# Seven-product FFN blocks: additions moved behind conversions, weight units taken earlier, two down products in the middle

## The chip, the cores and the metric

The kernel runs on one core of a Trainium2 chip. The metric is device time in microseconds (us) of one execution. TensorE (PE) multiplies, VectorE (DVE) and ScalarE (ACT) do elementwise work, SyncE (SP) issues the loads of weights.

## The reference

Two networks follow each other on x of 256 tokens by 1024. The first is an S5 block and an attention block. The second has two layers, each of an FFN, a hybrid mixer and another FFN:

```python
def swiglu(x, w_gate, w_up, w_down):
    return (jax.nn.silu(x @ w_gate) * (x @ w_up)) @ w_down
...
for l in range(DEPTH):
    x = x + 0.5 * swiglu(rmsnorm(x, ffn1_norm[l]), ffn1_w_gate[l], ffn1_w_up[l], ffn1_w_down[l])
    h = rmsnorm(x, mix_norm[l])
    x = x + hybrid_mixer(h, w_in[l], ...)
    x = x + 0.5 * swiglu(rmsnorm(x, ffn2_norm[l]), ffn2_w_gate[l], ffn2_w_up[l], ffn2_w_down[l])
return rmsnorm(x, final_norm)
```

The change is in the four FFNs: 1024 to 2816 and back to 1024, all in f32.

## The kernel before

**Products in three passes.** Every f32 operand is split into a high part (`whi`, written by ACT with a rounding copy, line 191) and a low part (`wlo`, what the copy left over, a subtraction on DVE, line 203). A product is then three matmuls on PE: high by high (line 280), then one with each low part (lines 281 and 282; in the FFN line 281 is the one that needs `wlo`).

**Units.** Weights come in units of 2048 columns per partition in all: four ACT copies of 512 and two DVE subtractions of 1024. `converting` is a generator over all units of the program; a step (a quarter) is one ACT copy, and the subtractions follow with a lag. `convert(n)` runs n steps, but stops once the unit after next is ready (`self.ready > self.taken + 2 - self.held`). `whi` and `wlo` have four buffers each, the loaded weights (`raw`) three. `take` hands over the next unit.

**Slots.** The program's order is written slot by slot. `K.slot` first issues the tasks due in the slot (on ACT and DVE), with `conv` conversion steps spread between them, and then the slot's matmuls with transposes (`pe`) at given places among them. An engine runs its instructions in the order issued here.

**An FFN.** The 2816 hidden columns are 11 blocks of 256. `BLOCKS = (1, 1, 1, 2, 1, 2, 1, 1, 1)` does seven blocks singly (`eight`: two slots of 24 matmuls) and twice a pair of blocks (`seven`): with sums and differences of the inputs (`xs`) and of four quarter blocks of weights (`Quad`, tiles `quad` and `mixed`, subtracted on DVE in `add`, line 168) seven products of 12 matmuls do the work of eight. Their sums are formed in the PSUM tiles a, b, c and, where two products share a tile, in SBUF: `sum11`, `sum22` and `sum12` (lines 581, 585, 589) are DVE additions. After a block is complete, `gated` makes silu(gate) on ACT (line 491) and multiplies on DVE (line 492), `turn` transposes on PE (line 498, tile `tph`), `divide` splits the result (tile `hh`), and a down product (`downs`, 24 matmuls into `acc`) adds it to the output. Down products of a block are done after the next block's `eight`, or inside the next `seven`: there the down product is cut in halves, one behind the fourth product and one behind the fifth.

The diff changes the order of all of these; the functions follow.

Of the kernel before, what the change touches and what calls it, by code (L numbers as in the profile page):

```python
# [14 lines left out]
ALU = mybir.AluOpType  # L15
# [3 lines left out]
P = 128  # L19
# [56 lines left out]
class Core:  # L76
# [20 lines left out]
    def f(self, shape, name, dtype=F32):  # L97
        return self.ap.tile(shape, dtype, tag="f", name=self.name(name), bufs=3)
# [132 lines left out]
        self.taken += 1  # L231
        return self.parts[i]

    def slot(self, mm, tasks=(), pe=(), conv=4):


        tasks = list(tasks)
        if conv > 2 and self.ready < self.taken + 2:
            conv += 2
        n = max(len(tasks), 1)  # L240
        done = 0
        for i in range(n):
            if i < len(tasks):
                tasks[i]()
            k = conv * (i + 1) // n
            self.convert(k - done)
            done = k
        if conv < 4:
            self.flush()
        pe = sorted(pe, key=lambda x: x[0])  # L250
        at = 0
        for _ in mm:
            while pe and pe[0][0] <= at:
                pe.pop(0)[1]()
            at += 1
        for _, f in pe:
            f()
# [187 lines left out]
BLOCKS = (1, 1, 1, 2, 1, 2, 1, 1, 1)  # L445


def ffn_units(w_gate, w_up, w_down):
    def quarter(j, k):
        cs = slice(j * 256, (j + 1) * 256)  # L450
        return [(0, w_gate[k * P:(k + 4) * P, cs]), (256, w_up[k * P:(k + 4) * P, cs])]

    out, j, due = [], 0, []
    assert sum(BLOCKS) == w_gate.shape[1] // 256 and BLOCKS[:2] == BLOCKS[-2:] == (1, 1)
    for b in BLOCKS:
        down = [(2, D, [(0, w_down[d * 256:(d + 1) * 256, :])]) for d in due]
        if b == 1:
            out += [(4, 512, quarter(j, k)) for k in (0, 4)] + down
        else:
            f = Quad([[quarter(j + i, k) for i in range(2)] for k in (0, 4)])  # L460
            out += f[:4] + down[:1] + f[4:5] + down[1:] + f[5:]
        due = list(range(j, j + b))
        j += b
    return out + [(2, D, [(0, w_down[d * 256:(d + 1) * 256, :])]) for d in due]


def ffn(K, h, norm, n, nxt):
# [3 lines left out]
    nc = K.nc  # L471
    V = nc.vector
    p, hid, tp, parts = {}, {}, {}, {}
    acc = []
    ahead = [([], []) for _ in range(3)]

    def slot(mm, tasks=(), pe=(), **kw):
        t, x = ahead.pop(0)
        ahead.append(([], []))
        K.slot(mm, t + list(tasks), x + list(pe), **kw)  # L480

    def then(i, *tasks, pe=()):

        ahead[i][0].extend(tasks)
        ahead[i][1].extend(pe)

    def gated(j, t, src=None):
        s = p[j][t] if src is None else src
        o = K.t([P, 512], "hid") if src is None or src is p.get((j, t)) else src
        a, hid[j, t] = o[:, 0:256], o[:, 256:512]  # L490
        nc.scalar.activation(a, s[:, 0:256], AF.Silu, scale=norm.col[:, t:t + 1])  # L491
        V.scalar_tensor_tensor(hid[j, t], s[:, 256:512], norm.col05[:, t:t + 1], a, op0=ALU.mult, op1=ALU.mult)  # L492

    def turn(j, t):
        if j not in tp:
            tp[j] = K.psum("ps", [P, 2, 2, P], "tph")
        for k in range(2):
            nc.tensor.transpose(tp[j][:, k, t], hid[j, t][:, k * P:(k + 1) * P], K.ident)  # L498

    def divide(j):  # L500
        hh = K.f([P, 2, 2, T], "hh", F32R)
        K.split(hh[:, 0], hh[:, 1], tp[j].rearrange("p k t c -> p k (t c)"))
        parts[j] = hh[:, 0], hh[:, 1]

    def down(j, w, hf, t):
        for k in range(2):
            c0 = hf * 512
            K.mm3(acc[hf][t], [a[:, k, t * P:(t + 1) * P] for a in parts[j]], [a[:, k, c0:c0 + 512] for a in w],
                  j == 0 and k == 0, j == n - 1 and k == 1)
            yield  # L510

    def downs(j, w, order=((0, 0), (0, 1), (1, 0), (1, 1))):
        for hf, t in order:
            yield from down(j, w, hf, t)
# [4 lines left out]
    def x_(hf, t):  # L519
        return [a[:, 4 * hf:4 * hf + 4, t * P:(t + 1) * P] for a in norm.x]  # L520
# [14 lines left out]
    def mix(i):  # L535
        f, s = blocks()
        a, b, op = ((f[1][0], f[1][1], ALU.add), (s[0], f[0][0], ALU.subtract), (f[0][0], f[1][0], ALU.subtract),
                    (f[0][1], s[1], ALU.subtract))[i]
        V.tensor_tensor(s[i], a, b, op=op)
# [9 lines left out]
    def s_(i):  # L549
        return [a[:, i] for a in sums["x"]]  # L550

    def form(out, a, first=False):

        w = K.take()
        for k in range(4):
            K.mm3(out, [y[:, k] for y in a], [y[:, k] for y in w], first and k == 0, k == 3, not first)
            yield

    def eight(j, due):

        p[j] = K.pair()
        for kh in range(2):
            tasks, pe = [], []
            if j == 0 and kh == 0:
                pe = norm.begin(1)
            elif j == 0:
                tasks = [norm.col_, norm.half_col]
            slot(K.rows_of(p[j], norm.x, K.take(), 4 * kh, 4, kh == 0, kh == 1), tasks, pe,
                 conv=2 if j == 0 and kh == 0 else 4)
        places = (3, 5) if due else (5, 7)  # L570
        then(0, lambda: gated(j, 0), lambda: gated(j, 1), pe=[(x, lambda t=t: turn(j, t)) for t, x in enumerate(places)])
        then(1, lambda: divide(j))

    def seven(j, due):

        a, b, c = (K.psum("ps", [P, 512], "p") for _ in range(3))
        c11, u2 = K.t([P, 512], "hid"), K.t([P, 512], "hid")
        c22 = K.t([P, 512], "hid")

        def sum11():  # L580
            V.tensor_tensor(c11, c11, b, op=ALU.add)
            gated(j, 0, c11)

        def sum22():
            V.tensor_tensor(c22, c22, a, op=ALU.add)
            gated(j + 1, 1, c22)

        def sum12():
            V.tensor_tensor(u2, u2, c, op=ALU.add)
            gated(j + 1, 0, u2)  # L590

        def sum21():
            p[j, 1] = a
            gated(j, 1, a)

        slot(form(a, x_(0, 0), first=True))
        then(0, lambda: nc.scalar.copy(c11, a))
        slot(form(b, x_(1, 0), first=True))
        then(0, sum11)
        slot(form(c, s_(0), first=True))  # L600
        then(0, lambda: nc.scalar.copy(c22, c))
        slot(form(a, s_(1)))
        then(0, lambda: nc.scalar.copy(u2, a))
        w = K.take()
        K.held = 1
        if len(due) == 1:
            slot(downs(due[0], w, ((0, 0), (0, 1))))
        else:
            slot(downs(due[0], w))
            K.held = 0  # L610
        slot(form(a, s_(2)))
        then(0, sum22)
        if len(due) == 1:
            slot(downs(due[0], w, ((1, 0), (1, 1))))
            K.held = 0
        else:
            slot(downs(due[1], K.take()))
        slot(form(a, x_(1, 1)))
        then(0, sum21)
        slot(form(c, s_(3)))  # L620
        then(0, sum12, pe=[(2, lambda: turn(j, 0)), (2, lambda: turn(j, 1)), (4, lambda: turn(j + 1, 1)),
                           (6, lambda: turn(j + 1, 0))])
        then(1, lambda: divide(j), lambda: divide(j + 1))

    j, due = 0, []
    for b in BLOCKS[:-1]:
        if b == 1:
            eight(j, due)
            if j == 0:
                then(1, whole)  # L630
            elif j == 1:
                acc = [K.pair("acc", "acc") for _ in range(2)]
                then(0, lambda: mix(0), lambda: mix(1))
                then(1, lambda: mix(2), lambda: mix(3), mixed_high, mixed_low)
            for d in due:
                slot(downs(d, K.take()))
        else:
            seven(j, due)
        due = list(range(j, j + b))
        j += b  # L640
    j = n - 1
    eight(j, due)
    ahead[0] = ([], [])
    ahead[1] = ([], [])
    w = [K.take()]

    def turned():
# [1496 lines left out]
```

## Time and profile before

| | |
|---|---|
| median of 3 runs | 1431.38 us (1429.34 to 1433.12) |
| profiled execution | 1432.99 us, of which its span is 1431.0 us |
| PE busy | 1377.9 us (96%) |
| DVE busy | 1103.0 us (77%) |
| ACT busy | 814.4 us (57%) |
| mean granted TensorE clock | 0.989 |

Busy time is summed over stages with different limits. Ends of matmuls are modelled, so that PE's own pace is read from the starts of its instructions. In a timeline a row has start, duration, engine, line, operation, tiles (written<-read), shapes and, in brackets, the idle time of the engine before it and what ended this.

### The profile page before, as it was taken

To read this page: it belongs to the slowest core of one execution; us is meant where nothing else is said; L and a number is where in the kernel's file an instruction comes from. 1 tells how busy PE (TensorE), PEld (TensorE's weight loads), DVE (VectorE), ACT (ScalarE), POOL (GpSimd) and SP (SyncE) were. 2 spreads that over 40 slices of the span, in tenths; PEclk is the share of its full clock that TensorE was granted. 3 is DMA by queue.
4 is the path that set the end of the run, shared out by engine and by line. 5 is a ranking of instruction groups with operands and counts; after the bars stand their busy time and mean duration, and the time that the engine had idled before them with its cause. 6 is when DMAs were issued, how large, how long until landed. Compare 5 with 4: busy or idle time off the path is not lost.

```text
span 1431.0 us, 21193 instructions
## 1 busy us (share of the span) xinstructions
PE 1377.9 (96%) x8205; PEld 1151.2 (80%) x8205; DVE 1103.0 (77%) x1801; ACT 814.4 (57%) x1581; POOL 28.1 (2%) x35
## 2 busy tenths in 40 slices
PE   8988999999999999999999999999999999999996
PEld 7877888988778899888877788787889887878775
DVE  7889887668886589777878747887669987688854
ACT  6525657665655474555565636566557564656552
POOL 0003200000000000000000000000000000000000
PEclk9999999999999999999999999999999999999998
DMA  8133655466446454465726556473645445646260
GB/s 211 63 123 104 213 172 154 139 199 215 150 144 235 148 177 141 132 196 164 257 80 214 186 169 203 150 236 98 228 131 191 147 170 170 213 147 230 85 215 29
DMA packets 181347, 237.16 MB, mean 166 GB/s; under 512 B 16952, under 2 KB 140144, under 8 KB 181248
## 3 DMA queue, kind: packets, MB, share of 16 engines
q1 hardware_dynamic: 180160, 233.47, 50.2%
q0 software_dynamic: 672, 1.81, 0.4%
q8 instruction: 64, 1.05, 0.3%
q10 hardware_dynamic: 416, 0.55, 0.1%
q14 instruction: 35, 0.29, 0.1%
HBM read 234.76 MB, written 1.05 MB: 165 GB/s over the span
## 4 chain that ended last, share of the span: by engine, by line
PE 79%; DVE 12%; DMA 2%; issue 2%; ACT 2%; SPq 0%; DVEq 0%; ACTq 0%
PE p L280 15%; PE p L281 15%; PE p L282 15%; PE acc L281 5%; PE acc L282 5%; PE acc L280 5%; DVE wlo L203 4%; PE g L281 2%; PE g L280 2%; PE g L282 2%; DVE quad L168 2%; DMA raw<-in_ffn_w_up_dram 1%; PE lv L1712 1%; PE tph L498 1%; PE g L764 1%
## 5 line engine op out<-in xcount | busy, mean ns | idle before, releaser
L191 ACT CAST whi<-raw 128x512 fp32r<-128x512 f32 x688 | 381.7, 619 | 151.3 <-PE p L282 81.7
L203 DVE TENSOR_TENSOR wlo<-raw,whi 128x1024 fp32r<-128x1024 f32 x344 | 410.5, 1217 | 7.6 <-ACT whi L191 7.2
L280 PE MATMUL p<-whi,xghi 128*128 128x512 f32 x800 | 319.9, 400 | 0.0
L281 PE MATMUL p<-wlo,xghi 128*128 128x512 f32 x800 | 312.8, 391 | 0.3
L282 PE MATMUL p<-whi,xglo 128*128 128x512 f32 x800 | 312.5, 391 | 0.0
L281 PEld LDWEIGHTS p<-wlo,xghi 128*128 128x128 f32 x800 | 150.5, 188 | 32.6 <-DVE wlo L203 3.6
L282 PEld LDWEIGHTS p<-whi,xglo 128*128 128x128 f32 x800 | 150.2, 188 | 32.1
L280 PEld LDWEIGHTS p<-whi,xghi 128*128 128x128 f32 x800 | 150.3, 188 | 29.0
L281 PE MATMUL acc<-wlo,hh 128*128 128x512 f32 x352 | 141.8, 403 | 15.4 <-DVE wlo L203 15.4
L280 PE MATMUL acc<-whi,hh 128*128 128x512 f32 x352 | 144.5, 410 | 0.0
L282 PE MATMUL acc<-whi,hh 128*128 128x512 f32 x352 | 140.7, 400 | 0.0
L191 ACT CAST whi<-quad 128x512 fp32r<-128x512 f32 x192 | 107.9, 617 | 52.3 <-DVE quad L168 29.7
L203 DVE TENSOR_TENSOR wlo<-quad,whi 128x1024 fp32r<-128x1024 f32 x96 | 113.6, 1217 | 0.0
L281 PEld LDWEIGHTS acc<-wlo,hh 128*128 128x128 f32 x352 | 67.6, 192 | 34.1 <-DVE wlo L203 22.3
L492 DVE SCALAR_TENSOR_TENSOR hid<-p,col,hid 128x256 f32<-128x256 f32 x64 | 30.8, 481 | 68.7 <-ACT hid L491 68.6
L282 PEld LDWEIGHTS acc<-whi,hh 128*128 128x128 f32 x352 | 67.5, 192 | 15.6 <-DVE hh L294 1.7
L280 PEld LDWEIGHTS acc<-whi,hh 128*128 128x128 f32 x352 | 67.2, 191 | 13.9 <-ACT hh L293 1.6
L294 DVE TENSOR_TENSOR hh<-tph,hh 128x512 fp32r<-128x512 f32 x44 | 30.4, 691 | 58.6 <-ACT hh L293 58.2
L280 PE MATMUL g<-xghi,whi 128*128 128x256 f32 x256 | 73.8, 288 | 0.0
L282 PE MATMUL g<-xghi,wlo 128*128 128x256 f32 x256 | 72.4, 283 | 0.0
L281 PE MATMUL g<-xglo,whi 128*128 128x256 f32 x256 | 72.4, 283 | 0.0
L764 PE MATMUL g<-xg,raw 128*128 128x256 f32 x256 | 61.0, 395 | 5.5 <-DVE kt L1043 3.6
(377 smaller groups left out, 2249.1 us busy)
## 6 DMA issues: line engine op xcount, KB each, us to landing
raw<-in_ffn_w_down_dram SPq DMA_DIRECT2D x44, 1024.0 KB, 4.9
raw<-in_w_in_dram SPq DMA_DIRECT2D x36, 1024.0 KB, 5.1
raw<-in_ffn_w_gate_dram SPq DMA_DIRECT2D x56, 512.0 KB, 4.1
raw<-in_ffn_w_up_dram SPq DMA_DIRECT2D x56, 512.0 KB, 5.2
raw<-in_attn_w_in_dram SPq DMA_DIRECT2D x16, 1024.0 KB, 5.6
quad<-in_ffn_w_gate_dram SPq DMA_DIRECT2D x32, 512.0 KB, 9.2
quad<-in_ffn_w_up_dram SPq DMA_DIRECT2D x32, 512.0 KB, 8.7
raw<-in_w_out_dram SPq DMA_DIRECT2D x8, 1024.0 KB, 5.1
```

Source lines behind the costliest of these rows:

```text
L168: self.nc.vector.tensor_tensor(u.buffer(self)[:, sl], a, b, op=ALU.subtract)
L191: self.nc.scalar.copy(hf[:, sl], raw[:, sl])
L203: self.nc.vector.tensor_tensor(out, raw, hi.bitcast(F32), op=ALU.subtract)
L280: nc.tensor.matmul(out, ah, bh, start=start, stop=False, skip_group_check=more)
L281: nc.tensor.matmul(out, ah, bl, start=False, stop=False, skip_group_check=more)
L282: nc.tensor.matmul(out, al, bh, start=False, stop=stop, skip_group_check=more)
L294: self.nc.vector.tensor_tensor(lo, x, hi.bitcast(F32), op=ALU.subtract)
L492: V.scalar_tensor_tensor(hid[j, t], s[:, 256:512], norm.col05[:, t:t + 1], a, op0=ALU.mult, op1=ALU.mult)
L498: nc.tensor.transpose(tp[j][:, k, t], hid[j, t][:, k * P:(k + 1) * P], K.ident)
L764: nc.tensor.matmul(us[s][:, m], ws[s][:, k, m * P:(m + 1) * P], xg[:, k], start=k == 0, stop=k == KC - 1)
L1712: nc.tensor.matmul(o, e[:, sl], e[:, sl], start=True, stop=True)
```

## The change

Four edits, all of order:

- `slot` takes a list `late`: the tasks of the slot are issued first, then half of its conversion steps, then the late tasks with the other half. `sum11`, `sum22`, `sum12` and the gating of the fourth output (`sum21`) become late tasks.
- Slots of an FFN have `conv=8` instead of 4 (or 6), and `seven` takes a unit ahead of its slot's conversions instead of behind them, so that conversions run one unit further ahead.
- `sum22` no longer reads a from PSUM: ACT copies a into a new tile u3 first.
- `kept_back`: of the down products due ahead of a `seven`, the last stays back, so that every `seven` has two whole down products in its middle and the `eight` before it one less behind it. Where none is left behind an `eight`, its transposes move into the second slot of the `seven`. The loads of the down weights move behind those of the quads.

```diff
-    def slot(self, mm, tasks=(), pe=(), conv=4):
+    def slot(self, mm, tasks=(), pe=(), conv=4, late=()):
         tasks = list(tasks)
-        if conv > 2 and self.ready < self.taken + 2:
+        if late:
+            for f in tasks:
+                f()
+            self.convert(conv // 2)
+            tasks = list(late)
+            conv -= conv // 2
+        if 2 < conv <= 4 and self.ready < self.taken + 2:
             conv += 2
...
+def kept_back(i, due):
+    return due[-1:] if i + 1 < len(BLOCKS) and BLOCKS[i + 1] == 2 else []
...
         if b == 1:
-            out += [(4, 512, quarter(j, k)) for k in (0, 4)] + down
+            kept = kept_back(i, due)
+            out += [(4, 512, quarter(j, k)) for k in (0, 4)] + down[:len(due) - len(kept)]
...
-        due = list(range(j, j + b))
+        due = kept + list(range(j, j + b))
...
-    def slot(mm, tasks=(), pe=(), **kw):
+    def slot(mm, tasks=(), pe=(), conv=8):
...
-        places = (3, 5) if due else (5, 7)
-        then(0, lambda: gated(j, 0), lambda: gated(j, 1), pe=[(x, lambda t=t: turn(j, t)) for t, x in enumerate(places)])
-        then(1, lambda: divide(j))
+        gates, turns = [lambda: gated(j, 0), lambda: gated(j, 1)], [lambda: turn(j, 0), lambda: turn(j, 1)]
+        then(0, *gates)
+        if n_downs:
+            then(0, pe=list(zip((3, 5), turns)))
+            then(1, lambda: divide(j))
...
+        else:
+            then(1, pe=list(zip((1, 2), turns)))
+            then(2, lambda: divide(j))
...
-            V.tensor_tensor(c22, c22, a, op=ALU.add)
+            V.tensor_tensor(c22, c22, u3, op=ALU.add)
...
-        slot(form(b, x_(1, 0), first=True))
-        then(0, sum11)
+        slot(form(b, x_(1, 0), K.take(), True))
+        then(0, late=[sum11])
...
-        slot(form(a, s_(2)))
-        then(0, sum22)
+        slot(form(a, s_(2), K.take()))
+        copy(u3, a)
+        then(0, late=[sum22])
```

Three places show what moves. Line numbers of the changed kernel are larger (581 is 601 there, 492 is 506, 498 is 512).

**DVE, first block of seven products of the first FFN, around `sum11`** (tile `hid_480`, after the change `hid_474`). Before:

```order
L168 TENSOR_TENSOR mixed_475_3758<-quad_444_3543,quad_441_3534 128x1024
L203 TENSOR_TENSOR wlo_473_3750<-quad_441_3534,whi_472_3749 128x1024 x2
L581 TENSOR_TENSOR hid_480_3795<-hid_480_3795,p_478_3793 128x512
L492 SCALAR_TENSOR_TENSOR hid_480_3795<-hid_480_3795,col05_432_3483 128x256
L203 TENSOR_TENSOR wlo_485_3815<-mixed_475_3758,whi_484_3814 128x1024
L168 TENSOR_TENSOR quad_443_3540<-quad_444_3543,quad_443_3540 128x1024
```

After:

```order
L203 TENSOR_TENSOR wlo_480_3757<-mixed_470_3717,whi_479_3756 128x1024
L168 TENSOR_TENSOR quad_436_3498<-quad_437_3501,quad_436_3498 128x1024
L203 TENSOR_TENSOR wlo_480_3757<-mixed_470_3717,whi_479_3756 128x1024
L301 TENSOR_TENSOR hh_485_3807<-tph_484_3796,hh_485_3807 128x512
L168 TENSOR_TENSOR quad_436_3498<-quad_437_3501,quad_436_3498 128x1024
L203 TENSOR_TENSOR wlo_483_3782<-raw_443_3541,whi_482_3781 128x1024 x2
L601 TENSOR_TENSOR hid_474_3749<-hid_474_3749,p_472_3747 128x512
L506 SCALAR_TENSOR_TENSOR hid_474_3749<-hid_474_3749,col05_432_3484 128x256
```

The addition waits for the block's second product (`p_478`, now `p_472`). The conversions of the fourth unit (`mixed`), of the fifth's first difference and of a down unit stood behind it or later and now stand ahead of it.

**DVE, ahead of the same block, around the gating of the single block before it** (tiles `hid_478` and `hid_481`, its two halves), after the change:

```order
L506 SCALAR_TENSOR_TENSOR hid_478_3753<-p_461_3667,col05_432_3484,hid_478_3753 128x256
L168 TENSOR_TENSOR mixed_470_3717<-quad_437_3501,quad_434_3492 128x1024
L203 TENSOR_TENSOR wlo_469_3712<-quad_434_3492,whi_468_3711 128x1024 x2
L506 SCALAR_TENSOR_TENSOR hid_481_3765<-p_462_3668,col05_432_3484,hid_481_3765 128x256
L203 TENSOR_TENSOR wlo_480_3757<-mixed_470_3717,whi_479_3756 128x1024
```

Before, two operations stood between the two halves; now three do, and the stretch of conversions ahead of them is another one, since the down unit that was converted there comes later.

**PE, second product of the same block, after the change** (`p_472` is b; `tph_484` takes the transposes of the single block before):

```order
L512 MATMUL tph_484_3796<-ident_67,hid_478_3753 128x128 x2
L287 MATMUL p_472_3747<-whi_464_3672,xghi_410_3345 128x512
L288 MATMUL p_472_3747<-wlo_465_3673,xghi_410_3345 128x512
L289 MATMUL p_472_3747<-whi_464_3672,xglo_411_3346 128x512
L512 MATMUL tph_484_3796<-ident_67,hid_481_3765 128x128 x2
```

These transposes stood between the matmuls of the down product that came ahead of the block; that product now stands inside the block, and they stand behind the second product's sixth and ninth matmul.

## Rows read from the trace of the kernel before

**Rows 1.** The profile's page: span, and busy time of each engine.

```profile
span 1431.0 us, 21193 instructions
PE 1377.9 (96%) x8205; PEld 1151.2 (80%) x8205; DVE 1103.0 (77%) x1801; ACT 814.4 (57%) x1581; POOL 28.1 (2%) x35
```

**Rows 2.** Windows: two of eight seven-product blocks, the eight's sum, a stretch inside.

```profile
349.06:379.15 30.09, 27.42 (x109) 20.96 (x108) 23.74 (x25) 17.95 (x34) 0.00 (x0) 0.94 0.11 36
402.44:431.33 28.89, 26.25 (x110) 19.81 (x108) 24.14 (x25) 17.96 (x34) 2.12 (x4) 1.00 0.19 66
sum 236.44, PE 215.12 PEld 163.30 DVE 191.56 ACT 143.65 POOL 4.24; mean PE 26.89 PEld 20.41 DVE 23.94 ACT 17.96 POOL 0.53
361.26:367.94 6.68, 4.76 (x13) 3.17 (x12) 6.64 (x6) 3.76 (x7) 0.00 (x0) 0.74 0.36 100
```

**Rows 3.** Waits, whole program: us in total, times, longest us.

```profile
PE acc L281 <- DVE wlo L203: 15.4, 16, 1.3
PE tph L498 <- DVE hid L492: 2.0, 3, 0.8
DVE hid L581 <- PE p L282: 16.1, 8, 3.1
DVE hid L585 <- PE p L282: 19.4, 8, 3.1
ACT whi L191 <- PE p L282: 88.9, 36, 3.5
```

**Rows 4.** Timeline, TensorE, first block: start us, duration us, what.

```profile
343.10 0.39 PE L280 MATMUL acc<-whi,hh 128*128 128x512 f32 x1
349.06 0.39 PE L280 MATMUL p<-whi,xghi 128*128 128x512 f32 x1
...
362.27 0.50 PE L281 MATMUL acc<-wlo,hh 128*128 128x512 f32 x1 [0.61 <-DVE wlo L203]
...
364.55 0.80 PE L281 MATMUL acc<-wlo,hh 128*128 128x512 f32 x1 [1.31 <-DVE wlo L203]
...
367.94 0.39 PE L280 MATMUL p<-whi,xshi 128*128 128x512 f32 x1
...
370.66 0.39 PE L280 MATMUL acc<-whi,hh 128*128 128x512 f32 x1
```

**Rows 5.** Timeline, VectorE, same stretch.

```profile
354.79 0.69 DVE L581 TENSOR_TENSOR hid<-hid,p 128x512 f32<-128x512 f32 x1 [2.23 <-PE p L282]
356.06 0.48 DVE L492 SCALAR_TENSOR_TENSOR hid<-hid,col 128x256 f32<-128x256 f32 x1 [0.58 <-ACT hid L491]
356.46 1.22 DVE L203 TENSOR_TENSOR wlo<-mixed,whi 128x1024 fp32r<-128x1024 f32 x1
357.60 1.22 DVE L168 TENSOR_TENSOR quad<-quad,quad 128x1024 f32<-128x1024 f32 x1
...
365.55 2.35 DVE L203 TENSOR_TENSOR wlo<-quad,whi 128x1024 fp32r<-128x1024 f32 x2
```

**Rows 6.** Timeline, VectorE, ahead of that block.

```profile
321.59 0.69 DVE L294 TENSOR_TENSOR hh<-tph,hh 128x512 fp32r<-128x512 f32 x1 [3.32 <-ACT hh L293]
...
331.65 0.69 DVE L294 TENSOR_TENSOR hh<-tph,hh 128x512 fp32r<-128x512 f32 x1
...
335.52 2.29 DVE L547 TENSOR_TENSOR xslo<-xs,xshi 128x2048 fp32r<-128x2048 f32 x1 [0.85 <-ACT xshi L543]
```

**Rows 7.** Groups by line: busy us, mean ns, idle before.

```profile
L203 DVE TENSOR_TENSOR wlo<-raw,whi 128x1024 fp32r<-128x1024 f32 x344 | 410.5, 1217 | 7.6 <-ACT whi L191 7.2
```

**Rows 8.** Timeline, ScalarE then TensorE, behind a second block.

```profile
1370.33 1.14 ACT L191 CAST whi<-raw 128x512 fp32r<-128x512 f32 x2 [2.07 <-DMA raw<-in_ffn_w_up_dram]
...
1372.41 0.44 PE L498 MATMUL tph<-ident,hid 128*128 128x128 f32 x2 [0.81 <-DVE hid L492]
```

**Rows 9.** Page, DMA issues: KB each, median us to landing.

```profile
raw<-in_ffn_w_down_dram SPq DMA_DIRECT2D x44, 1024.0 KB, 4.9
quad<-in_ffn_w_gate_dram SPq DMA_DIRECT2D x32, 512.0 KB, 9.2
```

More of the change, by code (lines that the diff above doesn't have):

```diff
@@ L454, in ffn_units @@
     assert sum(BLOCKS) == w_gate.shape[1] // 256 and BLOCKS[:2] == BLOCKS[-2:] == (1, 1)
-    for b in BLOCKS:
+    for i, b in enumerate(BLOCKS):
         down = [(2, D, [(0, w_down[d * 256:(d + 1) * 256, :])]) for d in due]
+        kept = []
         if b == 1:
-            out += [(4, 512, quarter(j, k)) for k in (0, 4)] + down
+            kept = kept_back(i, due)
+            out += [(4, 512, quarter(j, k)) for k in (0, 4)] + down[:len(due) - len(kept)]
         else:
@@ L474, in ffn, with then @@
     acc = []
-    ahead = [([], []) for _ in range(3)]
-    def slot(mm, tasks=(), pe=(), **kw):
[L478 to L485, printed above, removed]
+    ahead = [([], [], []) for _ in range(3)]
+    def slot(mm, tasks=(), pe=(), conv=8):
+        t, x, late = ahead.pop(0)
+        ahead.append(([], [], []))
+        K.slot(mm, t + list(tasks), x + list(pe), conv, late)
+    def then(i, *tasks, pe=(), late=()):
+        for x, y in zip(ahead[i], (tasks, pe, late)):
+            x.extend(y)
     def gated(j, t, src=None):
@@ L550, in s_, with form @@
         return [a[:, i] for a in sums["x"]]
-    def form(out, a, first=False):
-        w = K.take()
+    def form(out, a, w, first=False):
         for k in range(4):
@@ L557, in form, with eight @@
             yield
-    def eight(j, due):
+    def eight(j, n_downs):
         p[j] = K.pair()
@@ L568, in eight @@
             slot(K.rows_of(p[j], norm.x, K.take(), 4 * kh, 4, kh == 0, kh == 1), tasks, pe,
-                 conv=2 if j == 0 and kh == 0 else 4)
-        places = (3, 5) if due else (5, 7)
-        then(0, lambda: gated(j, 0), lambda: gated(j, 1), pe=[(x, lambda t=t: turn(j, t)) for t, x in enumerate(places)])
-        then(1, lambda: divide(j))
+                 conv=2 if j == 0 and kh == 0 else 8)
+        gates, turns = [lambda: gated(j, 0), lambda: gated(j, 1)], [lambda: turn(j, 0), lambda: turn(j, 1)]
[3 more added lines that the diff above has]
+            then(1, lambda: divide(j))
+        elif j == 0:
+            then(0, pe=list(zip((5, 7), turns)))
+            then(1, lambda: divide(j))
+        else:
+            then(1, pe=list(zip((1, 2), turns)))
+            then(2, lambda: divide(j))
     def seven(j, due):
         a, b, c = (K.psum("ps", [P, 512], "p") for _ in range(3))
-        c11, u2 = K.t([P, 512], "hid"), K.t([P, 512], "hid")
-        c22 = K.t([P, 512], "hid")
+        c11, u2, c22, u3 = (K.t([P, 512], "hid") for _ in range(4))
         def sum11():
@@ L594, in sum21, with copy @@
             gated(j, 1, a)
-        slot(form(a, x_(0, 0), first=True))
-        then(0, lambda: nc.scalar.copy(c11, a))
-        slot(form(b, x_(1, 0), first=True))
-        then(0, sum11)
[L600 to L603, printed above, removed]
+        def copy(dst, src):
+            then(0, lambda: nc.scalar.copy(dst, src))
+        slot(form(a, x_(0, 0), K.take(), True))
+        copy(c11, a)
+        slot(form(b, x_(1, 0), K.take(), True))
+        then(0, late=[sum11])
+        slot(form(c, s_(0), K.take(), True))
+        copy(c22, c)
+        slot(form(a, s_(1), K.take()))
+        copy(u2, a)
         w = K.take()
-        K.held = 1
+        halves = (((0, 0), (0, 1)), ((1, 0), (1, 1)))
         if len(due) == 1:
-            slot(downs(due[0], w, ((0, 0), (0, 1))))
+            K.held = 1
+            slot(downs(due[0], w, halves[0]))
         else:
             slot(downs(due[0], w))
-            K.held = 0
-        slot(form(a, s_(2)))
-        then(0, sum22)
+        slot(form(a, s_(2), K.take()))
+        copy(u3, a)
+        then(0, late=[sum22])
         if len(due) == 1:
-            slot(downs(due[0], w, ((1, 0), (1, 1))))
+            slot(downs(due[0], w, halves[1]))
             K.held = 0
@@ L617, in seven @@
             slot(downs(due[1], K.take()))
[L618 to L622, printed above, removed]
+        slot(form(a, x_(1, 1), K.take()))
+        then(0, late=[sum21])
+        slot(form(c, s_(3), K.take()))
+        then(0, late=[sum12], pe=[(2, lambda: turn(j, 0)), (2, lambda: turn(j, 1)), (4, lambda: turn(j + 1, 1)),
+                           (7, lambda: turn(j + 1, 0))])
         then(1, lambda: divide(j), lambda: divide(j + 1))
     j, due = 0, []
-    for b in BLOCKS[:-1]:
+    for i, b in enumerate(BLOCKS[:-1]):
         if b == 1:
-            eight(j, due)
+            kept = kept_back(i, due)
+            eight(j, len(due) - len(kept))
             if j == 0:
@@ L634, in ffn @@
                 then(1, lambda: mix(2), lambda: mix(3), mixed_high, mixed_low)
-            for d in due:
+            for d in due[:len(due) - len(kept)]:
                 slot(downs(d, K.take()))
@@ L638, in ffn @@
             seven(j, due)
-        due = list(range(j, j + b))
+            kept = []
+        due = kept + list(range(j, j + b))
         j += b
     j = n - 1
-    eight(j, due)
-    ahead[0] = ([], [])
-    ahead[1] = ([], [])
+    eight(j, 1)
+    ahead[0] = ([], [], [])
+    ahead[1] = ([], [], [])
     w = [K.take()]
```

## Prediction

> **What bounds the kernel now.** I read the page first, then the waits, then windows and timelines of the stretch that the change touches. On the page PE is busy for 96% of the span and the next engine, DVE, for 77% [rows 1]: a gain must come out of the gaps of PE. The waits say where those are: PE in a down product waits for the low part of weights, `wlo`, in 16 waits of up to 1.3 us [rows 3]. Sixteen is two for each of the eight blocks of seven products (two in each of four FFNs), so I went there.
>
> The price of a block comes from its windows. Twelve matmuls without a gap take 370.66 - 367.94 = 2.72 us [rows 4], 0.2267 us each. A block before the change has 7 products and one down product, 9 x 12 = 108 matmuls, so 24.5 us. The first takes 30.09 us, the second 28.89, all eight 236.44 [rows 2]: 236.44 - 8 x 24.48 = **40.6 us** are lost in the eight blocks. I use this difference and not the idle times of the waits, which start at modelled ends of matmuls and come out smaller.
>
> The two shown blocks differ by 1.2 us and in the granted clock, 0.94 against 1.00; the stretch behind the long waits has 0.74 [rows 2], so the clock there was at 1.2 instead of 2.4 GHz for a part. That came after gaps of PE that ended at 362.27 and 364.55 [rows 4]. It is a consequence of the waits, and in the sum above.
>
> Why is `wlo` late? DVE is busy for only 23.74 of 30.09 us [rows 2]. Its timeline shows `sum11` (L581) waiting 2.23 us for a product of PE, and the multiplication behind it another 0.58 us for ACT [rows 5]. DVE runs its queue in order, so the conversions behind these two stand still. From 356.46 to the end of the pair at 365.55, about 367.9, DVE then runs without a gap, in steps of 357.60 - 356.46 = 1.14 us per 1024 columns [rows 5] (1217 ns each, which overlap a little [rows 7]), and PE waits for it. Later `sum22` (L585) does the same: 19.4 us in 8 waits, `sum11` 16.1 in 8 [rows 3]. So DVE is idle while work for PE is behind it in its queue, then it is the bound for 11 us.
>
> **The change, part by part.**
>
> *Late additions.* Half of the slot's conversions go ahead of `sum11`, which is asked for at the end of the second product. In the new order six conversions or differences stand between the previous gating and it, 6 x 1.14 = 6.8 us: DVE reaches it when its product is done. Worth, per block: the 2.23 us of idle time and what follows from it. The 0.58 us for ACT stays; it delays everything behind it once.
>
> *Two whole down products instead of one.* PE gets 24 matmuls more in the block, 5.4 us, and DVE the two low parts of one more unit, 2 x 1.14 = 2.3 us. Over the FFN nothing is added, since both are missing behind the single block ahead. In the block it gives DVE 5.4 - 2.3 = 3.1 us in which to catch up.
>
> *Units taken ahead.* Conversion runs one unit further ahead. Nothing costs PE here as long as buffers are free; an ACT copy into the fourth buffer waits for the product that reads it (88.9 us in 36 waits already now [rows 3]), and what stands behind it in ACT's queue waits too. The gating's second half is such an instruction: it now stands behind four copies instead of two, two steps of 0.5 us later.
>
> *The copy u3.* Eight ACT copies more in the program, half a us each, in slots in which ACT (17.95 of 30.09 us [rows 2]) has room: nothing. Without that room it would delay the copies behind it by that half us.
>
> *The moved transposes: a new wait.* Where no down product is left ahead of the first block of an FFN, the transposes of the single block before come after the sixth and ninth matmul of the second product. I count when DVE has their input. Before, the block before ended at 343.10 [rows 4]; the new order puts the seven products there. The last event that the change doesn't move is the `hh` of 321.59, over at 322.2 [rows 6]. From there to the second half of the gating the new order has 16 operations of 1024 columns (18.2 us at 1.14), four of 512 and one `hh` (0.6 us each, 3.1), three multiplications (0.4 each by 356.46 - 356.06 [rows 5], 1.2) and the 2048-wide `xslo` (2.2): 24.7 us. Two waits remain: until 331.65 for the next `hh`, which DVE now reaches 0.6 us early, and 0.85 for `xshi` [rows 6]. So it starts at 322.2 + 24.7 + 1.4 = 348.3 and ends at 348.8. PE asks for it after 12 + 9 matmuls and a pair of transposes: 343.10 + 21 x 0.2267 + 0.15 = 348.0. PE waits **0.8 us**. A DVE without those two waits would give 0, one that is a further 2 us late 2.8.
>
> Then DVE has, without a gap, two low parts and two differences of 1024, one `hh` and the down unit's two low parts, 6 x 1.14 + 0.6: the second of these is done at about 356.2. PE wants it after three more matmuls, two products and four matmuls of the down product: 355.1 + 0.9 = 356.0. That is 0.2 to 0.3 us late; counting on through `sum11` and four conversions, the second down unit is as late again. I take 1.4 us for the first block of an FFN. Ahead of the second block a down product remains, and by the same count its units are 1 to 2 us early; I take 0.4 there. Per FFN 1.8 us, in the program 4 x 1.8 = **7.2 us** of waits that come or stay.
>
> *Behind the second block.* There the gating stands behind a copy that waits 2.07 us for weights, and PE's transposes wait 0.81 us for it [rows 8]; 2.0 us in three such waits [rows 3]. With units converted earlier the loads are asked for earlier. I take half, 1.0 us, between 0 and 2.
>
> *The loads.* In SP's queue the held down unit now stands behind eight loads of the quads. A load lands 4.9 us after its issue, one of a quad 9.2 [rows 9]. The quads must be there for the block's first products; the down unit is wanted four products, 10.9 us, after the first of these, so I take nothing. Without that room a copy would wait, as in the slower rival below.
>
> The sum, on the profiled execution's 1433.0 us (1.6 above the median of the three runs): 1433.0 - 40.6 - 1.0 + 7.2 = 1398.6; against the median, **1397 us**. Waits at zero everywhere would give 1431.4 - 40.6 - 2.0 = 1389.
>
> **The rivals.**
>
> *DVE stays late.* For it: from the gating to the end of the block DVE has some 20 operations in a row without a gap, and each us by which it starts late is a us of PE in the block; the gaps may again bring the clock down. Against it: DVE is busy for 79% of a block now. If it is 2 us later than counted in all eight blocks, 16 us of the gain go: 1413. It decides against the forecast from a second gating half at 350 on.
>
> *Nothing moves, since it isn't the order.* What would make this so is a buffer: if `wlo` were late because its four buffers free up late, the order would not matter and the time stay 1431. The 88.9 us of copies that wait for PE [rows 3] speak for it. Against it speaks that DVE's conversions run gap to gap from 356.46 and wait for no buffer [rows 5]. The Trainium skill has this as a rule (Perfetto Trace Analysis, Optimization Strategy): the same gap repeated on the engine that should be full can mean too few SBUF or PSUM buffers. Our gap repeats eight times, but the rows name a late operand, so by the trace the rule does not hold for these gaps.
>
> *Slower: the weights come late.* The second block's down units are loaded behind all its quads, and those wait until the first block has let go of its own. If a down unit landed after its slot began, ACT's whole queue would stand behind its copy. Its buffer comes free when the single block's first unit is converted, and its copy is due three slots of 24 matmuls and a product later, 3 x 5.44 + 2.72 = 19 us, against 9.2 us for a load among others [rows 9]. To lose, each of eight blocks must wait 34.4 / 8 = 4.3 us, so a load must take over 23 us. Every further us costs 8: at 25 us the time is 1397 + 8 x 6 = 1445.
>
> **How the numbers follow.** The forecast (1389 to 1404) has 0.66, DVE late (1404 to 1418) 0.22, a smaller gain from both 0.04, nothing 0.05, slower 0.03. The likeliest case gives 1397. The range 1388 to 1412 leaves out less than 2 in 10: its lower end is all waits gone, its upper DVE late by nearly 2 us in each block. Differences of under 0.3%, 4 us, are about what a measurement of this kernel can't tell from none. Faster by more: 0.92; within: 0.05; slower: 0.03.
>
> **What would show it.** In the profile after, `sum11` and `sum22` should have no wait for PE, and the 15.4 us of PE in down products for `wlo` should fall under 4. A window of a block, now 132 matmuls or 29.9 us, should take 30 to 32 us, at a granted clock of 1.00. PE's transposes should show four waits for the multiplication of about 0.8 us, one per FFN, in the first blocks; were these 2 us or more, or the clock still lower there, the count of DVE's operations is wrong. Waits of ACT for loads of down weights over 2 us would be the third rival.

## The result and the profile after

The changed kernel takes 1394.28 us (median of 4 runs, 1393.96 to 1396.21); the kernel before, run beside it, 1432.22 us. The ratio is 0.9741, with a 95% interval of 0.9724 to 0.9759. By the ratio it is faster by 37 us. The forecast was 1397 us.

The page after, span and busy times; its profiled execution took 1394.2 us:

```profile
span 1392.1 us, 21232 instructions
PE 1360.4 (98%) x8205; PEld 1148.8 (83%) x8205; DVE 1101.1 (79%) x1801; ACT 817.5 (59%) x1589; POOL 27.4 (2%) x35
```

Against [rows 1] the span is 38.9 us shorter, DVE has as much work as before (1101.1 us) and ACT has 8 instructions more, the copies u3. PE runs as many instructions as before. What was saved is waiting, and the stretches at the lower clock that came with it.

Windows of the eight blocks of seven products, each from its first matmul to the first one behind it (duration, busy time of PE, PEld, DVE, ACT and POOL, then clock, DMA share, GB/s). A block now has 132 matmuls, 29.92 us without a gap:

```profile
341.32:373.20 31.88, 31.13 (x138) 24.89 (x136) 30.72 (x32) 23.36 (x45) 0.00 (x0) 1.00 0.40 131
391.10:421.04 29.94, 29.94 (x133) 24.77 (x132) 28.39 (x28) 22.69 (x43) 2.12 (x4) 1.00 0.27 83
697.10:729.02 31.92, 31.17 (x138) 24.90 (x137) 30.77 (x32) 23.39 (x45) 0.00 (x0) 1.00 0.41 129
746.90:776.84 29.94, 29.94 (x133) 24.78 (x132) 28.39 (x28) 22.68 (x43) 0.00 (x0) 1.00 0.26 82
880.86:912.77 31.91, 31.19 (x138) 24.89 (x136) 30.75 (x32) 23.38 (x45) 0.00 (x0) 1.00 0.41 131
930.64:960.58 29.94, 29.94 (x134) 24.77 (x133) 28.40 (x28) 22.70 (x43) 2.12 (x4) 1.00 0.26 83
1236.69:1268.56 31.87, 31.15 (x138) 24.90 (x137) 30.71 (x32) 23.36 (x45) 0.00 (x0) 1.00 0.40 131
1286.42:1316.88 30.46, 30.44 (x134) 24.63 (x133) 28.43 (x28) 23.02 (x44) 0.00 (x0) 1.00 0.24 71
sum 247.86, PE 244.90 PEld 198.54 DVE 236.55 ACT 184.58 POOL 4.24; mean PE 30.61 PEld 24.82 DVE 29.57 ACT 23.07 POOL 0.53
```

Three of the four second blocks have almost no gap left (0.02 us over 29.92). Every window has the clock 1.00, where the first of [rows 2] had 0.94. And DVE is now busy for 30.72 of 31.88 us in a first block: it has room of about a microsecond.

Waits of TensorE over the whole program (us in total, times, longest):

```profile
PE tph L512 <- DVE hid L506: 3.1, 5, 0.7
PE yps L1090 <- issue: 0.6, 2, 0.4
```

The second row is the shortest that this view gives; a down product's wait for `wlo`, 15.4 us in [rows 3], is no longer among its rows. The waits for the gating have grown in number, from 3 to 5: the four new ones that were forecast, and one of the three old ones. TensorE, second product of the first block:

```profile
346.09 0.39 PE L289 MATMUL p<-whi,xglo 128*128 128x512 f32 x1
347.21 0.44 PE L512 MATMUL tph<-ident,hid 128*128 128x128 f32 x2 [0.73 <-DVE hid L506]
347.40 0.48 PE L287 MATMUL p<-whi,xghi 128*128 128x512 f32 x1
...
348.18 0.40 PE L287 MATMUL p<-whi,xshi 128*128 128x512 f32 x1
```

VectorE, same stretch, to be read beside [rows 5]:

```profile
346.68 0.47 DVE L506 SCALAR_TENSOR_TENSOR hid<-p,col,hid 128x256 f32<-128x256 f32 x1
347.07 1.21 DVE L203 TENSOR_TENSOR wlo<-mixed,whi 128x1024 fp32r<-128x1024 f32 x1
...
352.21 2.35 DVE L203 TENSOR_TENSOR wlo<-raw,whi 128x1024 fp32r<-128x1024 f32 x2
354.48 0.68 DVE L601 TENSOR_TENSOR hid<-hid,p 128x512 f32<-128x512 f32 x1
355.74 0.48 DVE L506 SCALAR_TENSOR_TENSOR hid<-hid,col 128x256 f32<-128x256 f32 x1 [0.58 <-ACT hid L505]
356.14 1.22 DVE L203 TENSOR_TENSOR wlo<-quad,whi 128x1024 fp32r<-128x1024 f32 x1
```

`sum11` (L601) has no bracket: its 2.23 us of waiting for PE are gone. It now starts 6.3 us after the next product began at 348.18, so the product that it adds is long done; the 0.58 us behind it for ACT stayed.

**Where the time came from.** The eight windows exceed 8 x 29.92 us by 8.5 us. Of these, 16 transposes, which stood outside the block before, are 1.9: eight pairs of 0.23 us each (from 341.32 to 346.09 there are 20 steps of 0.2267 us and one pair). So 6.6 us are lost where 40.6 were: 34.0 us. Behind the second blocks, the next 96 matmuls with their transposes take 93.6 us in the four FFNs together, where they took 96.5: 2.9 us. That is 36.9 of the 38.9 us by which the span fell. Of the other 2.0 us, 1.8 were gained ahead of the first block (it starts at 341.32, and before, the down product in that place started at 343.10). They need not come from the change: in the run with both gating halves early (below), whose order up to this block is the same, it starts at 343.77.

### The profile page after: what moved, and what is told of

It reads as the page before. It is cut to its first block, busy times and chain, and to the rows that moved or that the text cites. A ratio compares the mean times of both kernels' runs of the same rounds, so it can differ in the third digit from the quotient of the medians.

```text
span 1392.1 us, 21232 instructions
## 1 busy us (share of the span) xinstructions
PE 1360.4 (98%) x8205; PEld 1148.8 (83%) x8205; DVE 1101.1 (79%) x1801; ACT 817.5 (59%) x1589; POOL 27.4 (2%) x35
## 5 line engine op out<-in xcount | busy, mean ns | idle before, releaser
L287 PE MATMUL acc<-whi,hh 128*128 128x512 f32 x352 | 141.7, 402 | 0.0
L288 PE MATMUL acc<-wlo,hh 128*128 128x512 f32 x352 | 138.7, 394 | 0.1
L289 PE MATMUL acc<-whi,hh 128*128 128x512 f32 x352 | 138.1, 392 | 0.0
L289 PEld LDWEIGHTS acc<-whi,hh 128*128 128x128 f32 x352 | 66.1, 188 | 15.4 <-DVE hh L301 1.7
```

Of the source, the lines that this page charges most:

```text
L287: nc.tensor.matmul(out, ah, bh, start=start, stop=False, skip_group_check=more)
L288: nc.tensor.matmul(out, ah, bl, start=False, stop=False, skip_group_check=more)
L289: nc.tensor.matmul(out, al, bh, start=False, stop=stop, skip_group_check=more)
```

## Experiments

The three parts were first made alone on the kernel before, then taken out of the kernel after one at a time, and then the one surprise was taken apart. Ratios are to the kernel before:

| kernel | median us | ratio (95% interval) |
|---|---|---|
| before + late additions only | 1416.35 | 0.9897 (0.9880 to 0.9915) |
| before + two whole down products only | 1416.69 | 0.9900 (0.9882 to 0.9918) |
| before + further reach only | 1410.04 | 0.9852 (0.9835 to 0.9869) |
| after without late additions | 1397.25 | 0.9766 (0.9747 to 0.9784) |
| after, unit taken behind its slot's conversions | 1411.12 | 0.9861 (0.9840 to 0.9883) |
| after without u3 | 1397.87 | 0.9766 (0.9751 to 0.9781) |
| after, halves of one down product | 1422.90 | 0.9942 (0.9925 to 0.9958) |
| the same, copy of a ahead of four casts | 1411.68 | 0.9866 (0.9851 to 0.9880) |
| the same, additions ahead of conversions | 1412.57 | 0.9865 (0.9849 to 0.9882) |
| after, both gating halves early | 1395.64 | 0.9750 (0.9735 to 0.9765) |

The theory was that the order of DVE's queue makes `wlo` late. The main rival was that DVE has too much to do in a block whatever the order, the other that buffers decide.

**Late additions alone.**

```diff
-        then(0, sum11)
+        then(0, late=[sum11])
```

(and the same for `sum22`, `sum21` and `sum12`, with `late` in `slot` as in the change.)

> The kernel before with one edit: the four additions of a seven-product block go behind half of their slot's conversions; order of units, reach of the conversions and down products as before. Theory (DVE idles at the head of its queue for sum11, and its conversions are late for it): the 2.2 us of waiting ahead of sum11 become about 0, the waits of PE in a block fall from 4.4-5.6 to about 2.5 us, the time to 1408-1415. Rival (VectorE has too much to do in the block, whatever the order): the waits of PE stay, 1428-1432.

It gained 15 us, and at 1416 us lies 1 us above the theory's range. Its waits of TensorE:

```profile
PE acc L288 <- DVE wlo L203: 15.3, 16, 1.3
PE tph L505 <- DVE hid L499: 0.4, 1, 0.4
```

The wait for `wlo` in down products is as large as in [rows 3], and yet the blocks were 27.5 us where 28.9 and 30.1 were (three with a fallen clock 28.8). The transposes' wait for the gating fell from 2.0 us to 0.4. What went inside the blocks is a gap of 0.8 us (from start to start) in the fourth product, ahead of those in the down product. The waits of before have it in a row that [rows 3] leaves out, and this run does not have it:

```profile
PE p L281 <- DVE wlo L203: 4.8, 8, 0.6
```

The down product's waits stayed although `sum11` waits for nothing now. VectorE in the first block, first a row of before, then three of this run:

```profile
361.00 1.22 DVE L203 TENSOR_TENSOR wlo<-raw,whi 128x1024 fp32r<-128x1024 f32 x1
```

```profile
353.24 0.68 DVE L588 TENSOR_TENSOR hid<-hid,p 128x512 f32<-128x512 f32 x1
...
358.40 1.22 DVE L203 TENSOR_TENSOR wlo<-raw,whi 128x1024 fp32r<-128x1024 f32 x1
...
360.67 1.22 DVE L203 TENSOR_TENSOR wlo<-raw,whi 128x1024 fp32r<-128x1024 f32 x1
```

The down unit's first low part is made 2.6 us earlier, but PE comes to it 2.6 us earlier too (its wait ends at 359.67, in [rows 4] at 362.27). DVE runs without a gap from 355.00 on, and between the two low parts it still makes a difference of quads. So the idle time of DVE at `sum11` cost time, but not in the row on which I had put it.

**Two whole down products alone.**

```diff
-            out += [(4, 512, quarter(j, k)) for k in (0, 4)] + down
+            kept = kept_back(i, due)
+            out += [(4, 512, quarter(j, k)) for k in (0, 4)] + down[:len(due) - len(kept)]
```

> The kernel before with one edit: two whole down products in the middle of every seven-product block, one less behind the single block ahead. Theory (order of VectorE's queue): VectorE still idles for sum11, and the block now begins 5.4 us of TensorE earlier against 2.3 us of VectorE's work saved, so the waits move to its first half and the gain is small: 1420-1432. Rival (balance of work in the block is what counts): 3.1 us per block come back, 1404-1410.

It gained 14 us, more than my range and less than the rival's. Its waits of TensorE:

```profile
PE p L281 <- DVE wlo L203: 8.5, 8, 1.5
PE acc L281 <- DVE wlo L203: 6.2, 16, 0.6
```

The waits in down products fell to 6.2 us, and one of 1.1 us on average stays per block, in a product. More matmuls in the middle help, but not enough. DVE's waits at `sum11` (L592 here):

```profile
DVE hid L592 <- PE p L282: 7.3, 4, 2.2
```

DVE still stops at `sum11` in four blocks, the second ones. In the first blocks it no longer does, and they take even longer (33.6 us against 32.6): they begin 5.4 us of PE's work earlier, and DVE is spared only the 2.3 us of one down unit. So neither theory alone gives the 37 us.

**Further reach alone.**

```diff
-        slot(form(a, s_(2)))
+        slot(form(a, s_(2), K.take()))
...
-                 conv=2 if j == 0 and kh == 0 else 4)
+                 conv=2 if j == 0 and kh == 0 else 8)
```

(all seven products, and `conv=8` in all slots of an FFN.)

> The kernel before with one edit: in seven-product blocks the unit is taken ahead of the slot's conversions, and slots of an FFN convert up to 8 steps, so that conversions run one unit further ahead. Theory: VectorE has 2 to 4 operations more ahead of sum11 and reaches it when the second product is done, its idle time ahead of sum11 falls under 0.5 us, and most of the gain comes from this edit alone: 1398-1408. Rival (moving the additions is what counts): sum11 still blocks, 1424-1432.

It gained 21 us, the most of the three and 2 us short of the theory's range, though the additions stand where they stood in the slot. As the theory said, DVE waits for PE at `sum11` in no block any more. Waits of TensorE:

```profile
PE acc L281 <- DVE wlo L203: 7.1, 8, 1.3
PE p L280 <- ACT hid L602: 5.4, 8, 0.7
```

The second row is new, and no step of mine had it: the fifth product goes into the PSUM tile a again, and PE must wait until ACT has copied a away (L602). In ACT's queue four casts stand before that copy, as before, but with conversions further ahead they are those of a later unit: in the first block they wait for the differences that DVE begins at 360.88 and 363.15, where before they waited for those of 357.60 and 359.87.

**After without the late additions.**

```diff
-        then(0, late=[sum11])
+        then(0, sum11)
```

> The kernel after without its late additions: sum11, sum22, sum21 and sum12 stand ahead of all conversions of their slot, all else as after. Theory: with the conversions a unit further ahead VectorE reaches sum11 some 4.5 us earlier than now, still after the product that it waits for, so this edit alone is worth little here: 1393-1400. Rival (late additions are the source of the gain): the waits of 2 us per block come back, 1408-1420.

It is 3 us slower than after, with overlapping intervals. Waits of TensorE:

```profile
PE tph L512 <- DVE hid L506: 3.1, 5, 0.7
PE acc L288 <- DVE wlo L203: 1.2, 2, 1.1
```

DVE doesn't wait for PE at `sum11` here either. In the first block its order is even the same as in the kernel after, up to `sum22`: with conversions a unit ahead, those that `sum11` could hold up already stand ahead of it. The late additions, worth 15 us alone, are worth some 3 on top of the others.

**After, with the unit taken behind its slot's conversions.**

```diff
-    def form(out, a, w, first=False):
+    def form(out, a, take, first=False):
+        w = take()
...
-        slot(form(a, s_(2), K.take()))
+        slot(form(a, s_(2), K.take))
```

(all seven products; `form` starts behind the slot's conversions.)

> The kernel after, but a product of a seven-product block takes its unit behind its slot's conversions, as before (8 steps at most per slot stay): the conversions run a unit less far ahead in the block. Theory: less reserve ahead of the additions, waits of up to 1.5 us per block: 1396-1406. Rival: no part of the gain, 1393-1396.

It is 17 us slower than after, more than my range (its upper end was 1406). Waits of TensorE:

```profile
PE acc L288 <- DVE wlo L203: 13.9, 16, 2.3
```

The old wait is back, two per block, though the late additions stand in this kernel. The reach is what keeps `wlo` in time in down products.

**After without u3** (`sum22` reads a from PSUM).

```diff
-        copy(u3, a)
...
-            V.tensor_tensor(c22, c22, u3, op=ALU.add)
+            V.tensor_tensor(c22, c22, a, op=ALU.add)
```

> The kernel after, where sum22 reads the tile a from PSUM again and the copy into u3 is gone. Theory: the sixth product may not write a before sum22 has read it, and sum22 now stands late in VectorE's queue, so TensorE waits 0.5 to 2 us ahead of the sixth product in each of eight blocks: 1398-1410. Rival (VectorE is early enough, the copy only costs ScalarE): 1393-1396.

It is 3 to 4 us slower than after, just below the theory's range, and again its interval overlaps that of after. Waits of TensorE:

```profile
PE p L287 <- DVE hid L605: 2.0, 5, 0.4
```

The sixth product, into a, now waits for `sum22` (L605). The copy costs ACT 8 instructions and spares PE this wait.

**After with halves of one down product**, as before the change.

```diff
-    return due[-1:] if i + 1 < len(BLOCKS) and BLOCKS[i + 1] == 2 else []
+    return []
```

> The kernel after without the held-back down products: one down product per seven-product block, in halves, the other behind the single block ahead, as before; late additions and the further reach of conversions stay. Theory: VectorE lacks the 3.1 us per block in which to catch up, part of the waits come back at the low parts of the down unit and of the fifth product: 1398-1412. Rival (order alone is enough): 1393-1397.

The surprise: 1422.9 us, 11 above the upper end of the theory, and 13 above the further reach alone, though it has that and more. Waits of TensorE:

```profile
PE p L287 <- ACT hid L617: 15.1, 8, 2.3
```

It isn't `wlo`; it is the copy of a again (L617 here), three times as long. ScalarE around the wait in the first block; PE starts the fifth product at 364.42:

```profile
360.55 0.51 ACT L505 ACTIVATE hid<-hid,rs 128x256 f32<-128x256 f32 x1 [2.86 <-DVE hid L601]
360.96 0.57 ACT L617 COPY hid<-p 128x512 f32<-128x512 f32 x1
361.43 1.14 ACT L191 CAST whi<-quad 128x512 fp32r<-128x512 f32 x2
362.74 1.14 ACT L191 CAST whi<-quad 128x512 fp32r<-128x512 f32 x2 [0.18 <-DVE quad L168]
363.79 0.57 ACT L617 COPY hid<-p 128x512 f32<-128x512 f32 x1
```

Read from the bottom: the copy at 363.79 is what PE waits for. Ahead of it stand four casts, ahead of these a copy and the silu (L505) that waited 2.86 us for `sum11` on DVE. `sum11` is late because it is behind conversions. Only 12 matmuls of the half down product, 2.7 us, lie on PE between the product and its next use of a. Two runs took this chain apart.

**The same, with the copy of a ahead of the four casts.** The fourth product's slot converts nothing, so that its casts come behind the copy:

```diff
-        slot(form(a, s_(1), K.take()))
+        slot(form(a, s_(1), K.take()), conv=-1)
...
-        if conv < 4:
+        if 0 <= conv < 4:
```

> The kernel after with halves of one down product (1422.9 us), and the copy of a after the fourth product placed on ACT ahead of the four casts of a quad that stood before it. Theory (the 2.2 us before the second product into a is the cover of 12 matmuls being too short for a copy that stands behind four casts, themselves behind DVE's quad): the wait of PE for ACT's copy, 15.1 us in all, falls under 5 us, and the time to 1404 to 1412 us, with some of it coming back as waits of acc or p for wlo since the casts are later. Rival (half a down product less in the middle is too little work for DVE's lists, whatever stands on ACT): the wait goes over into waits for wlo of the same size, 1418 to 1424 us.

It gained 11 us, at the upper end of the theory's range. ScalarE in the same place, then TensorE's waits:

```profile
361.95 0.51 ACT L505 ACTIVATE hid<-hid,rs 128x256 f32<-128x256 f32 x1 [2.86 <-DVE hid L601]
362.37 1.05 ACT L617 COPY hid<-p 128x512 f32<-128x512 f32 x2
363.31 4.26 ACT L191 CAST whi<-quad 128x512 fp32r<-128x512 f32 x8
```

```profile
PE p L288 <- DVE wlo L203: 8.4, 8, 1.3
PE tph L512 <- DVE hid L609: 4.1, 8, 0.5
```

Both copies now run together, the wait for them is gone, and 8.4 us of it came back as a wait of the same product for `wlo`, as the theory allowed. Not all of the 11 us is the shorter wait: the granted clock fell in three blocks of the kernel with halves and in none here, which is some 5 us (last section).

**The same, with the additions ahead of the conversions.**

```diff
-        then(0, late=[sum11])
+        then(0, sum11)
```

> The kernel after with halves of one down product and with the four additions ahead of the conversions again. Theory (with the addition late on DVE, the silu behind it on ACT is late too, and the copies of the products queue behind that silu: the late additions are what makes halves cost more than in the kernel with only the further reach): as that kernel, 1407 to 1413 us, with the wait for the copy at about 5 us in all. Rival (the further copy and the other order of the tail make the difference, not the additions): 1418 to 1424 us.

It gained 10 us, within the theory's range, and is near the further reach alone (1412.57 against 1410.04 us, with overlapping intervals). Waits of TensorE:

```profile
PE acc L288 <- DVE wlo L203: 7.2, 8, 1.3
PE p L287 <- ACT hid L617: 5.4, 8, 0.7
```

These are that kernel's two rows, within 0.1 us. So where the down product is halved, late additions are a loss of 10 us, of which some 5 are again the clock: the silu behind `sum11`, and with it the copies, come late. With a whole down product there are 24 matmuls to hide it, and they are worth some 3 us.

**After, with both halves of the gating early**, where no down product is left behind the single block. It aims at the four waits of 0.9 us that remain.

```diff
-        then(0, *gates)
+        then(0, *(gates if n_downs or j == 0 else [lambda: [f() for f in gates]]))
```

> The kernel after, with both halves of the gating ahead of the conversions in the slot behind a single block that has no down product behind it, so that TensorE's transposes don't wait for the second half (0.89 us in the first block of each FFN). Theory (VectorE works gap to gap from there, the wait only moves): the 4 waits at the transposes go, and the low part of the first down unit is late by as much instead: 1392-1395. Rival (a wait of its own): 4 x 0.89 = 3.6 us less, 1390-1391.

It takes 1395.64 us: no gain, as the theory said. Waits of TensorE:

```profile
PE acc L288 <- DVE wlo L203: 2.3, 8, 0.4
```

The wait for the gating is out of the list and one for `wlo` is in it. DVE works without a gap there, so an operation put first makes another late. None of the versions is faster than the kernel after.

## Why the prediction was right, and where its steps were not

- **The 40.6 us.** Nearly all of it went, as forecast, and the blocks lose 6.6 us where 7.2 were forecast. The sum on the profiled execution was 1398.6 us, and it took 1394.2: of the 4.4 us, 0.6 are these, 1.9 lie behind the second blocks (below), and 2.0 lie elsewhere, most of them ahead of the first block.
- **The new wait at the transposes.** Forecast 0.8 us, in four places; between starts PE loses 0.88 to 0.89 us in each. The count held: DVE's second gating half was to begin 5.2 us after the block's start and began 5.4 after it (346.68 - 341.32), PE was to ask 4.9 us after it and did 5.0 after (346.09 + 0.23).
- **The other waits.** For the rest of a first block 0.6 us were forecast (1.4 less 0.8); the four take 0.6 more than the matmuls, the transposes and that wait. The second blocks were to lose 0.4 us each; three lose 0.02 and the last 0.54.
- **Behind the second blocks** 2.9 us came back, where I took 1.0 and at most 2. This is the largest error of a term, 1.9 us.
- **The cause.** The late additions were to be worth the idle time at `sum11` and what follows from it. Alone they gain 15 us, for 16.1 us of idle time [rows 3], and nothing beyond it. `sum22`, of which I said that it does the same, cost PE little: the 48 matmuls from 367.94 to 379.15 take 0.3 us more than without a gap. The three parts gain 15, 14 and 21 us alone, 50 together, and 37 in one kernel (without the clock some 40 and 32, last section). Left out of that kernel, the reach costs 17 and the down products 29 (in both, part is the clock's) and the additions 3. My list of terms did not show that the additions and the reach replace each other in large part.
- **The two down products** were costed as 3.1 us in which DVE catches up. They are also the cover for ACT's copy of a: of the 29 us that halves cost, 11 come back with the copy's place alone (some 5 of them by the clock). Of the 17 that remain, 8.4 show as the wait for `wlo` that I had named; waits of the transposes, 4.1 us in 8, are new beside it, and the rest I did not trace.
- **u3** was costed at nothing; without it the kernel is some 3 us slower, at the edge of what was measured.
- **The rivals.** *DVE stays late* didn't happen: the gating half was in place to 0.2 us. *Nothing moves* fell with the windows: the number of buffers is unchanged and all but 6.6 us of the gaps are gone. The Trainium skill's rule for the same gap repeated (Perfetto Trace Analysis, Optimization Strategy) therefore doesn't hold for the gaps before; for the wait for a in the halved kernel, which is a PSUM tile that isn't free yet, it points the right way, though there too an order of instructions gave 11 us (some 5 by the clock) without another buffer. *The weights come late* had a poor sign: waits of ACT for down weights over 2 us are there, but they mean nothing by themselves. ACT's waits after:

```profile
ACT whi L191 <- DMA raw<-in_ffn_w_down_dram: 10.3, 4, 3.4
```

They stand one in each FFN behind the second block, where conversions run so far ahead that they reach the load; only in the last does PE then lose 0.4 us at the transposes. The sign should have been a wait of PE for `whi` or `wlo` behind them.

## What to carry to other kernels

In DVE's and ACT's queues here an instruction that waits holds all that stands behind it; count from its place when each engine reaches it, as was done for the new wait, where it came out within 0.2 us. Gains of edits that pull the same work forward need not add up: try each alone and each left out before giving shares, and take the clock out of them. And when an operation is put back in one queue, follow what hangs on it through the next engine's queue (addition, silu, copy, the reused PSUM tile), and ask how many matmuls cover it.

## What was not expected of the hardware

The clock. Before, the starts of PE's matmuls show the same three gaps in all eight blocks (0.8, 0.8 and 1.5 us), and the granted clock fell to 1.2 GHz for 3.4 us behind them in four of the eight, two first and two second blocks. In the kernel with halves it fell in three first blocks, behind gaps of 2.4 us, and not in two other blocks with gaps of 2.4 and 2.5 us; with the unit taken behind its slot's conversions it fell in one of four blocks with a gap of 2.4 us; with halves and the copy moved, whose first blocks have a gap of 1.6 us, in none. Windows of the first block and of the fourth FFN's first block with halves, then of the first block with the copy moved:

```profile
348.44:377.07 28.63, 26.42 (x110) 21.33 (x109) 25.04 (x26) 20.11 (x39) 0.00 (x0) 0.94 0.12 38
1265.22:1292.20 26.98, 24.77 (x109) 20.19 (x108) 24.99 (x25) 20.05 (x38) 0.00 (x0) 1.00 0.11 39
```

```profile
349.85:376.10 26.25, 24.92 (x109) 20.20 (x108) 25.00 (x25) 19.96 (x38) 0.00 (x0) 1.00 0.13 41
```

So the same gaps cost a block 1.2 us or more on top [rows 2], or not, and what decides it these runs don't show. In four blocks that is 5 us, more than the late additions or u3 are worth in the kernel after. With halves it is 1.6 us a block, 5 us in three.

The clock therefore stands in the gains above. It fell in three blocks with late additions alone, and in none with two whole down products alone, with the further reach alone and in the kernel after. An estimate from these windows: of the 14, 21 and 37 us some 5 each are the clock, of the 15 some 1. Without it the three parts gain some 40 us together, against 32 in one kernel. The windows are of one execution each. The mean granted clocks of the others fit (0.988 to 0.993 before and 0.989 to 0.990 with halves, 0.993 to 0.995 in those three kernels; 0.989 to 0.994 with late additions alone, where the 1 us is the least certain). The reach's 17 us hold some of it too: with the unit taken behind its slot's conversions, four executions took 1409.3, 1409.4, 1412.9 and 1414.9 us at mean clocks of 0.993, 0.991, 0.990 and 0.989.
